# A new hand-laid order of the instructions on all five engines up to the last token tile, and a bit test of two transposes taken out, in a hybrid encoder layer on one core

## The chip, the cores and the metric

The kernel runs on one core of a Trainium2 chip. The metric is the device time of one execution in microseconds (us). Three runs of the kernel before gave 1298.33 us in the median (1297.25 to 1299.77). Everything that the engines do is in float32; a matmul is made of three passes over rounded high and low halves of its operands.

## The reference

One layer of an encoder is computed for nine token tiles: eight of 128 frames of a new stream, and one of 64 frames that continue a running stream with 512 cached positions.

```python
x <- LayerNorm(ALPHA * x + Mixer(x))          # D_MODEL = 1024
x <- LayerNorm(ALPHA * x + SqReLU_MLP(x))     # D_FF = 4096

Mixer: z = x @ w_in, its columns split among
  fox   6 heads x 64   causal softmax attention, logit += c_t - c_s, c = cumsum(log f)
  sgu   256 channels   u * (tril(W_s) @ LayerNorm(gelu(v)) + b) within 128 positions
  sb    6 heads x 64   strictly causal stick-breaking attention
  o = per-head RMSNorm of [fox, sgu, sb];  o @ w_out

def sq_relu_mlp(x, w_up, w_down):
    h = jnp.square(jax.nn.relu(x @ w_up))
    return h @ w_down
```

The new rows of keys, values and log gates are outputs too.

## The kernel before, in words

The program has four stages, one after the other but overlapping at their edges: the input projections with the two attentions and the gating (up to some 496 us of the profile), the output projection of one token tile after another, called mix (to some 607 us), the up projection, and the down projection, whose end also writes the outputs.

- **Projections.** `tok_mm` (L655) multiplies a transposed token tile `xT` by a slice of `w_in` into a PSUM bank. Its outputs are named `kvfox`, `qfox`, `kvsb`, `qsb`, `sgv` and so on. `x_trans` (L603) transposes the tiles of x that were loaded at L593 into buffers called `row_N`; `load_w` loads a weight slice (L624, `raw`) and splits it into halves (L628). The stores of new keys and values (L765, L766) come from `kvsfox`.
- **Attention.** A unit `b` is one head for one 256-row block of queries. Its scores `Sfox` or `Ssb` are made at L854, the row work follows on VectorE, ScalarE and GpSimd, and then the steps in `b_steps` run: `tr(m)` transposes blocks of weights into the PSUM tile `pt` (L903, the names `ptfox` and `ptsb`), VectorE splits `pt` into two halves `pth`, and `av(m)` multiplies these by the values into `ofox` or `osb` (L924 to L927). For two of the units, `fox1_1_0` and `sb1_1_0`, and only for m = 1, `tr` also makes a **test**: one block is transposed a second time in another number format (`same`, L907), VectorE takes the difference to the first, squares and sums it (`df`, L909 to L912), and adds the sum, times 2 to the 80th, to `negh` (L913), a small column that the unit uses elsewhere. Equal bits add zero.
- **Mix.** L522 multiplies the merged heads of one token tile by `w_out`; `ORD` gives the order of the tiles, the last one is tile 7. LayerNorm and the transposition for the MLP follow tile by tile (`row6`, `xr`, `xo`).
- **Up projection.** It runs as seven products of half-size blocks in place of eight (a Strassen-like scheme). A `Chain` (p, s) makes the seven products of weight block p with token half s: s = 0 has 288 columns, s = 1 has 256. Its banks are `zA_s`, `zB_s`, `zC_s`, `zD_s` (the matmuls at L1626), ScalarE copies `zA` out to `sn` (L1637), VectorE forms the others (L1640 to L1646), then come the squared relu (L1658), four block sums (L1667 to L1670) and stores to `h_dr` in memory (L1671, L1672). The weights of p = 0 are the first tiles `wa`, `ws`, `oTb`, `row1r`, `row4r`; those of each later p are loaded by one transfer `wr<-w_up` (L1826) and split by ScalarE (L1564, L1857), VectorE and GpSimd (L316).
- **Storage.** Big buffers lie in `row_N` places that are used again by later tiles. So `sn` of the chains after p = 0 lies where the `row` buffers of the last chain of p = 0, (0,1), lay: ScalarE can fill it only when the store of that buffer to `h_dr` has landed.

What sets the order: the program is recorded in full, and then each engine's instructions are chained in the order that the table `ORDER[engine]` gives, as words "n+k" (n times: take element k of those that are left). It is an order only, with no waiting beside it: an instruction starts when its engine has come to it and the data are there. SP's table orders the transfers that its queue issues, which stand behind each other in the same way.

Of the kernel before, what the change touches and what calls it, by code (L numbers as in the profile page):

```python
# [13 lines left out]
F32 = mybir.dt.float32  # L14
F32R = mybir.dt.float32r
AF = mybir.ActivationFunctionType
ALU = mybir.AluOpType
AX = mybir.AxisListType
# [3 lines left out]
P = 128  # L22
# [252 lines left out]
def _build(nc, tc, a, es):  # L275
# [23 lines left out]
    ident = cp.tile([P, P], F32, name="ident")  # L299
# [2207 lines left out]
```

## Time and profile before

| | |
|---|---|
| median of three runs | 1298.33 us |
| profiled execution, its own time | 1299.34 us |
| its span | 1297.6 us |
| TensorE (PE) busy | 1268.3 us, 98% |
| VectorE (DVE), ScalarE (ACT), GpSimd (POOL) busy | 966.8, 723.7, 602.5 us |
| mean granted TensorE clock | 0.995 |

The profiled execution is 1.0 us longer than the median, and 1.74 us of it lie outside the span. In the page, PE is the matmul engine, PEld its weight loads, which overlap, and SP the engine that issues most transfers (its queue is SPq in the trace). A timeline row gives the start in us, the time from the first start to the last end, the engine, the source line, the operation with its output and inputs, the shapes, the number of instructions in the row, and in brackets how long the engine had been idle and what released it. Matmuls are pipelined, so the start of one to the start of the next is the time that it takes.

### The profile page before, as it was taken

The page shows a single profiled execution, that of the slowest core. Times are in us where ns is not written, and L with a number is a line of the kernel's source. Part 1 is how long each engine was busy: PE and PEld are TensorE (multiplying, and loading weights), DVE is VectorE, ACT ScalarE, POOL GpSimd, SP SyncE. Part 2 cuts the span into 40 slices and gives each one's busy share as a digit, 9 for nine tenths or more (in the row PEclk, how much of TensorE's full clock was granted, in tenths as well). Part 3 has the DMA queues.
Part 4 walks back from the last instruction along what each step waited for, and adds up shares of the span by engine and source line. Part 5 has one row for each costly group of instructions (what it writes and reads, how often), then busy time and mean ns, then how long its engine had stood idle before and what let it go on. Part 6 is the DMA issues. An engine that isn't in the chain of part 4 may idle for free.

```text
span 1297.6 us, 24367 instructions
## 1 busy us (share of the span) xinstructions
PE 1268.3 (98%) x8853; PEld 1175.2 (91%) x8853; DVE 966.8 (75%) x1812; ACT 723.7 (56%) x1560; POOL 602.5 (46%) x670
## 2 busy tenths in 40 slices
PE   8999999999999999999899999999999999999996
PEld 8999999999989997778899999999988888888885
DVE  5678676778885687898678766766797667676777
ACT  4467676677675674344333222222367676676775
POOL 2232323257684666866122212121287656555567
PEclk9999999999999999999899999999999999999999
DMA  7445674322314376432324443535577443434433
GB/s 239 117 145 152 189 215 118 85 69 75 75 30 98 93 247 221 143 114 80 111 95 153 152 151 124 178 100 181 201 265 257 141 140 132 152 129 148 150 121 134
DMA packets 158049, 185.64 MB, mean 143 GB/s; under 512 B 27741, under 2 KB 116125, under 8 KB 157929
## 3 DMA queue, kind: packets, MB, share of 16 engines
q1 hardware_dynamic: 155832, 183.01, 44.5%
q8 instruction: 70, 1.15, 0.4%
q10 hardware_dynamic: 2096, 1.07, 0.3%
q14 instruction: 51, 0.41, 0.1%
HBM read 117.65 MB, written 60.10 MB: 137 GB/s over the span
## 4 chain that ended last, share of the span: by engine, by line
PE 79%; DVE 6%; POOL 5%; DMA 4%; issue 2%; ACT 2%; SPq 1%; DVEq 0%; POOLq 0%; ACTq 0%
PE A L2103 12%; PE zA L1626 11%; PE zD L1626 7%; PE D L2103 6%; PE kvsb L655 6%; PE kvfox L655 4%; PE zC L1626 4%; PE zB L1626 4%; PE B L2103 3%; PE Sfox L854 2%; PE mx L522 2%; PE qsb L795 2%; PE Ssb L854 2%; PE qfox L795 2%; PE sgu L655 1%
## 5 line engine op out<-in xcount | busy, mean ns | idle before, releaser
L316 POOL TENSOR_TENSOR wa<-wr,wa 128x512 fp32r<-128x512 f32 x41 | 56.6, 1403 | 233.1 <-ACT wa L1564 233.1
L316 POOL TENSOR_TENSOR wd<-rd,wd 128x512 fp32r<-128x512 f32 x77 | 104.0, 1361 | 109.2 <-ACT wd L1564 95.6
L1626 PE MATMUL zD<-xo,ws 128*128 128x288 f32 (+1 forms) x720 | 122.2, 287 | 0.1
L1626 PE MATMUL zA<-xo,ws 128*128 128x256 f32 (+1 forms) x720 | 113.1, 289 | 5.2 <-ACT sn L1637 5.2
L1626 PEld LDWEIGHTS zA<-xo,ws 128*128 128x128 f32 x720 | 99.5, 190 | 5.5 <-ACT sn L1637 5.5
L1626 PEld LDWEIGHTS zD<-xo,ws 128*128 128x128 f32 x720 | 102.9, 189 | 0.4 <-DVE hh L1640 0.4
L1637 ACT ACTIVATE sn<-zA 128x256 f32<-128x256 f32 (+1 forms) x80 | 30.8, 392 | 127.3 <-PE zA L1626 108.6
L522 PE MATMUL mx<-xT,oTb 128*128 128x512 f32 (+1 forms) x416 | 99.9, 394 | 1.0 <-DVE oTb L316 0.9
L655 PE MATMUL kvfox<-wkvfox,xT 128*128 128x256 f32 (+3 forms) x624 | 92.2, 289 | 2.5 <-DVE fx L758 1.3
L2103 PE MATMUL A<-wd,wd 128*128 128x512 f32 x312 | 94.2, 389 | 0.0
L522 PEld LDWEIGHTS mx<-xT,oTb 128*128 128x128 f32 (+1 forms) x416 | 75.6, 186 | 18.9 <-DVE oTb L316 1.7
L840 POOL TENSOR_TENSOR row<-row,row 128x127 f32<-128x127 f32 (+8 forms) x51 | 64.3, 1262 | 42.8 <-DVE row L838 34.2
L655 PEld LDWEIGHTS kvfox<-wkvfox,xT 128*128 128x128 f32 (+1 forms) x624 | 80.8, 187 | 3.1 <-DVE fx L758 1.5
L655 PE MATMUL kvsb<-wkvsb,xT 128*128 128x256 f32 (+1 forms) x624 | 79.7, 281 | 0.0
L1758 POOL TENSOR_TENSOR rd<-rd 128x512 f32<-128x512 f32 x56 | 73.3, 1310 | 10.1 <-DVE b L316 6.2
L2103 PE MATMUL A<-wd,h4a 128*128 128x512 f32 x240 | 77.7, 389 | 0.0
L838 DVE TENSOR_TENSOR_SCAN row<-row,one 128x128 f32<-128x128 f32 (+8 forms) x51 | 71.8, 1411 | 4.5 <-ACT row L837 3.4
L655 PEld LDWEIGHTS kvsb<-wkvsb,xT 128*128 128x128 f32 (+1 forms) x624 | 74.9, 186 | 0.0
L1564 ACT ACTIVATE wd<-rd 128x512 fp32r<-128x512 f32 x105 | 63.4, 621 | 17.3 <-POOL rd L1758 7.9
L2103 PEld LDWEIGHTS A<-wd,wd 128*128 128x128 f32 x312 | 58.6, 188 | 12.9
L2070 DVE TENSOR_TENSOR acc<-acc,A 128x512 f32<-128x512 f32 x73 | 49.6, 684 | 25.3 <-PE A L2103 24.8
L1626 PE MATMUL zB<-xo,wa 128*128 128x288 f32 (+1 forms) x360 | 66.5, 288 | 0.0
(729 smaller groups left out, 3861.6 us busy)
## 6 DMA issues: line engine op xcount, KB each, us to landing
h_dr<-hh SPq DMA_DIRECT2D x30, 512.0 KB, 3.2
rd<-w_down SPq DMA_DIRECT2D x30, 512.0 KB, 4.4
wr<-w_up SPq DMA_DIRECT2D x13, 1024.0 KB, 5.6
hr<-h_dr SPq DMA_DIRECT2D x31, 384.0 KB, 3.2
h_dr<-hh SPq DMA_DIRECT2D x30, 384.0 KB, 3.1
raw<-w_in SPq DMA_DIRECT2D x42, 256.0 KB, 3.2
wo_dr<-swo SPq DMA_DIRECT2D x32, 256.0 KB, 2.3
xT<-wo_dr SPq DMA_DIRECT2D x8, 1024.0 KB, 7.6
```

The lines of the kernel that those rows point to most:

```text
L316: eng.tensor_tensor(out, src, hi.bitcast(F32), op=ALU.subtract)
L522: nc.tensor.matmul(acc[0:m], oT[:, k, hx, 0:m], wo[k // 4][hw][:, k % 4, cs], start=(i == 0), stop=(i == len(seq) - 1))
L655: nc.tensor.matmul(acc[0:n, c0:c0 + n1 - n0], xT[k // 4][:, k % 4, c:c + n], wt[:, k, hw, n0:n1], start=(i == 0), stop=(i == len(seq) - 1))
L795: nc.tensor.matmul(acc[:, 0:w], wq[:, k, hw, :], xT[k // 4][:, k % 4, c:c + w], start=(i == 0), stop=(i == len(seq) - 1))
L838: nc.vector.tensor_tensor_scan(g[:, 0:n][:, ::-1], g[:, 0:n][:, ::-1], one.broadcast_to([P, n]), 1.0, op0=ALU.mult, op1=ALU.bypass)
L840: nc.gpsimd.tensor_tensor(s[:, 0:n - 1], s[:, 0:n - 1], g[:, 1:n], op=ALU.mult)
L854: nc.tensor.matmul(sps[:, b0 - c0:b0 - c0 + n], qd[:, h, s, half * P:(half + 1) * P], kp[b0 // 256][:, h, 0:n], start=(s == 0), stop=(s == ...
L1564: nc.scalar.activation(hi, raw, AF.Copy)
L1626: nc.tensor.matmul(z, w[:, hw, k], xop(s, bo, hx)[:, k, :], start=(new and k == 0 and j == 0), stop=(k == 3 and j == 2), skip_group_check= ...
L1758: eng.tensor_tensor(r[:, o], r[:, x], r[:, y], op=ALU.subtract)
L2070: nc.vector.tensor_tensor(out, out if other is None else other, bank, op=ALU.add)
L2103: nc.tensor.matmul(z, h[:, hx, q, o], wset[self.c % 2][q][:, hw, wb], start=((n in (0, 3) or n == 1 and self.c == 0) and q == 0 and j == 0 ...
```

## The change

The `ORDER` tables of all five engines are written anew, for the part of the program up to the last token tile. The rest of each table gives the order of before: from 706 us of the old profile on, every engine's order is the same. 5047 of the 8851 matmuls stand at another place, and 883 VectorE, 698 ScalarE, 341 GpSimd and 414 SP instructions do. The test in `tr` is gone, and with it two transpositions on PE and ten VectorE instructions. The changed file is six lines longer in all; lines behind the table are numbered 17 higher than before, and behind the test 6 higher.

```diff
 ORDER = {}
-14 2+10 +12 1 +11 2+9 1 +8 1 +7 21 +14 2+10 +12 3+10 1 +9 +33 +36 1 2+32 +33 +32 2 2+6 +28 1 7+5 +51 1 +46 +19
...
                         nc.tensor.transpose(ptr[:, bi * P:(bi + 1) * P], rows[half][1][:, kb * P:(kb + 1) * P], env["identr"])
-                    if nm in ("fox1_1_0", "sb1_1_0") and m == 1:
-                        at = len(traced)
-                        same = ps.tile([P, P], F32, name=f"same{nm}", tag="o", bufs=1)
-                        nc.tensor.transpose(same, rows[0][0][:, 2 * P:3 * P], ident)
-                        df = sa.tile([P, P + 1], F32, name=f"df{nm}", tag="df", bufs=1)
-                        nc.vector.tensor_copy(df[:, 0:P], same)
-                        nc.vector.tensor_tensor(df[:, 0:P], pt[:, 0:P], df[:, 0:P], op=ALU.subtract)
-                        nc.vector.tensor_tensor(df[:, 0:P], df[:, 0:P], df[:, 0:P], op=ALU.mult)
-                        nc.vector.tensor_reduce(df[:, P:P + 1], df[:, 0:P], axis=AX.X, op=ALU.add)
-                        nc.vector.scalar_tensor_tensor(negh, df[:, P:P + 1], 2.0 ** 80, negh, op0=ALU.mult, op1=ALU.add)
-                        apart.update(i.name for i in traced[at:])
...
-        left = [i for i in traced[from_here:] if i.engine == e.engine and "Boundary" not in type(i).__name__ and i.name not in apart]
+        left = [i for i in traced[from_here:] if i.engine == e.engine and "Boundary" not in type(i).__name__]
```

**The seam between the first weight block and the second, on PE.** In these names the first number behind `zB_`, `zA_` and so on is the half s. `oTb` and `row1r` are weights of p = 0 and `wa`, `ws` are weights of p = 1, and `xo` is the transposed input. Before, the last product of chain (0,1), zD, ends the work on p = 0:

```order
L1626 MATMUL zC_1_9013<-xo_8723,row1r 128x256 x4
L1626 MATMUL zD_1_8979<-xo_8722,oTb 128x256
L1626 MATMUL zA_1_9182<-xo_8722,wa_8922 128x256 x3
L1626 MATMUL zD_1_8979<-xo_8722,oTb 128x256 x11
L1626 MATMUL zA_1_9182<-xo_8722,wa_8922 128x256 x2
L1626 MATMUL zD_0_9119<-xo_7969,ws_9010 128x288 x2
L1626 MATMUL zB_0_9092<-xo_7969,wa_8922 128x288 x2
L1626 MATMUL zC_0_9146<-xo_7969,wa_8922 128x288
L1626 MATMUL zA_0_9076<-xo_7969,ws_9010 128x288
```

Now, from the same last product on:

```order
L1632 MATMUL zD_1_8963<-xo_8706,oTb 128x256 x12
L1632 MATMUL zC_0_9130<-xo_7953,wa_8906 128x288 x3
L1632 MATMUL zC_1_9249<-xo_8707,wa_8906 128x256 x2
L1632 MATMUL zB_0_9076<-xo_7953,wa_8906 128x288 x2
L1632 MATMUL zC_1_9249<-xo_8707,wa_8906 128x256
L1632 MATMUL zC_0_9130<-xo_7953,wa_8906 128x288
L1632 MATMUL zA_1_9166<-xo_8706,wa_8906 128x256
L1632 MATMUL zB_0_9076<-xo_7953,wa_8906 128x288
```

The row `zA_0<-xo,ws`, the third product of chain (1,0), stood 7 matmuls behind the last zD of p = 0; it now stands 61 matmuls behind it, and the matmuls between belong to the first products of both chains of p = 1 and to the parts of zB, zC and zD that need no `sn`.

**The same seam on VectorE.** `row_116` and `row_110` belong to chain (0,1), `h_0` to chain (0,0), `ws_9010` and `ws_8994` are weights of p = 1. Before:

```order
L316 TENSOR_TENSOR ws_9010<-row_92,ws_9010 128x8x128
L1642 TENSOR_TENSOR row_116<-zB_1_8952,sn_1_0_8929 128x256
L1646 TENSOR_TENSOR row_110<-zD_1_8979,sn_1_1_8930 128x256
L1658 SCALAR_TENSOR_TENSOR row_116<-row_116 128x512
L1658 SCALAR_TENSOR_TENSOR row_110<-row_110 128x512
L1668 TENSOR_TENSOR h_0_8798<-h_0_8798 128x256
L1667 TENSOR_TENSOR row_116<-row_110 128x256
L1668 TENSOR_TENSOR row_116<-row_116 128x256
L1669 TENSOR_TENSOR h_0_8798<-h_0_8798 128x256
L1670 TENSOR_TENSOR row_110<-row_116,row_110 128x256
L1669 TENSOR_TENSOR row_110<-row_116 128x256
```

Now:

```order
L1664 SCALAR_TENSOR_TENSOR row_116<-row_116 128x512
L1652 TENSOR_TENSOR row_110<-zD_1_8963,sn_1_1_8914 128x256
L1664 SCALAR_TENSOR_TENSOR row_110<-row_110 128x512
L1673 TENSOR_TENSOR row_116<-row_110 128x256
L1674 TENSOR_TENSOR row_116<-row_116 128x256
L1675 TENSOR_TENSOR row_110<-row_116 128x256
L1676 TENSOR_TENSOR row_110<-row_116,row_110 128x256
L1674 TENSOR_TENSOR h_0_8782<-h_0_8782 128x256
L333 TENSOR_TENSOR ws_8994<-row_80,ws_8994 128x8x128
L1675 TENSOR_TENSOR h_0_8782<-h_0_8782 128x256
```

The relu of `row_116` and its zB and zC sums moved ahead of the last zD, the two sums of `h_0` moved behind those of chain (0,1), and the two `ws` splits moved from ahead of these steps to behind them. On ScalarE, the transfer `wr<-w_up` of the next weight block stood behind the first copy `sn_0`; it now stands behind two copies, `sn_0` and `sn_1`.

**Transposes on PE.** The names `ptfox_2_1_0` and `ptfox_2_1_1` are blocks of one unit. Before, they stand one by one among the matmuls:

```order
L903 MATMUL ptfox_2_1_0_1521<-identr,row4r 128x128
L854 MATMUL Sfox_6_0_512_1588<-kpfox_3_553,qdfox_3_1130 128x128
L926 MATMUL ofox_2_0_1302<-pthfox_2_0_1_1367,vpfox_1_350 128x256
L927 MATMUL ofox_2_0_1302<-pthfox_2_0_1_1367,vpfox_1_350 128x256
L924 MATMUL ofox_2_0_1302<-pthfox_2_0_2_1411,vpfox_2_453 128x256
L925 MATMUL ofox_2_0_1302<-pthfox_2_0_2_1411,vpfox_2_453 128x128
L903 MATMUL ptfox_2_1_1_1549<-identr,row4r 128x128
L655 MATMUL kvfox_7_1485<-wkvfox_720,xT_181 128x256
```

Now:

```order
L871 MATMUL Sfox_7_0_512_1609<-kpfox_2_452,qdfox_3_1130 128x256 x2
L920 MATMUL ptfox_2_1_1_1549<-identr,row4r 128x128
L920 MATMUL ptfox_2_1_1_1549<-identr,row3r 128x128
L920 MATMUL ptfox_2_1_2_1572<-identr,row4r 128x128
L920 MATMUL ptfox_2_1_2_1572<-identr,row3r 128x128
L672 MATMUL kvfox_8_1814<-wkvfox_720,xT_181 64x256
```

Up to the last matmul of mix, the PE order of before has 399 runs of one or more transposes between matmuls, 200 of them a single transpose; the order of after has 329 runs, 155 of them single.

**The start of SP's queue.** `x_prompt` and `w_in` rows are loads; `p_fox_k` rows are stores of computed keys. Before:

```order
L593 DMA row_86<-x_prompt 128x1024
L593 DMA row_80<-x_prompt 128x1024
L624 DMA raw_0_244<-w_in 128x4x128
L678 DMA bf_654<-b_f 128x6
L678 DMA bf_908<-b_f 128x6
L624 DMA raw_1_248<-w_in 128x4x128
```

Now:

```order
L610 DMA row_86<-x_prompt 128x1024
L695 DMA bf_908<-b_f 128x6
L782 DMA p_fox_k<-kvsfox_0_294 128x128
L610 DMA row_116<-x_prompt 128x1024
L641 DMA raw_0_244<-w_in 128x4x128
L782 DMA p_fox_k<-kvsfox_1_341 128x128
L610 DMA row_80<-x_prompt 128x1024
L783 DMA p_fox_v<-kvsfox_0_294 128x128
L783 DMA p_fox_v<-kvsfox_1_341 128x128
L782 DMA p_fox_k<-kvsfox_2_397 128x128
```

The load of `row_80`, a later tile of x, now stands behind the stores of the first two computed key tiles.

410 rows, old and new, of the table ORDER are left out of this document.

## The prediction

> **What bounds the kernel now.** I read the page's busy shares first.
>
> ```profile
> PE 1268.3 (98%) x8853; PEld 1175.2 (91%) x8853; DVE 966.8 (75%) x1812; ACT 723.7 (56%) x1560; POOL 602.5 (46%) x670
> ```
>
> PE is the bound; no engine beside it is above 75%. A table by stage shows how much PE leaves open, and where (columns: length, then busy time of PE, PEld, DVE, ACT and POOL, the clock, the DMA share, GB/s).
>
> ```profile
> 0.00:607.00 607.00, 593.61 (x4660) 563.87 (x4661) 457.03 (x984) 369.87 (x882) 301.17 (x419) 1.00 0.45 131
> 635.00:647.00 12.00, 6.75 (x33) 6.52 (x32) 3.81 (x10) 0.67 (x2) 0.00 (x0) 0.72 0.70 230
> 647.00:706.00 59.00, 59.00 (x481) 59.00 (x480) 45.95 (x64) 17.62 (x33) 12.39 (x9) 1.00 0.38 123
> 706.00:1287.00 581.00, 580.87 (x3460) 518.56 (x3460) 426.99 (x698) 315.92 (x609) 274.57 (x225) 1.00 0.47 158
> ```
>
> From 647 us PE has no gap, and from 706 us nothing is moved. What a new order can win lies in two places: 607.00 - 593.61 = 13.4 us of idle PE up to 607, and 12.00 - 6.75 = 5.25 us in the 12 us at the seam of the first two weight blocks, where the clock is 0.72 besides. Busy time can shrink too, if the same matmuls follow each other at shorter distances. The waits of PE in 0 to 610 us (total, times, longest) are many and small: 23 rows, with a sum of 12.5 us, of which these matter.
>
> ```profile
> PE warm L1402 <- POOL ident masks.py:199: 1.6, 1, 1.6
> PE kvfox L655 <- DVE fx L758: 1.3, 1, 1.3
> PE kvfox L655 <- ACT wkvfox L628: 1.2, 1, 1.2
> PE osb L924 <- ACT osbsb L937: 1.0, 1, 1.0
> PE mx L522 <- DVE row3a L527: 0.2, 1, 0.2
> ```
>
> **A: the seam.** The timeline of PE, with those of ACT and POOL, the piece of the chain that PE waits for, and the transfers of `w_up` that follow (count, size, median us to land):
>
> ```profile
> 628.45 1.58 PE L1626 MATMUL zA<-xo,oTb 128*128 128x256 f32 x12
> 629.86 0.28 PE L1626 MATMUL zD<-xo,oTb 128*128 128x256 f32 x1
> ...
> 633.54 1.41 PE L1626 MATMUL zD<-xo,oTb 128*128 128x256 f32 x11
> 634.79 0.39 PE L1626 MATMUL zA<-xo,wa 128*128 128x256 f32 x2
> 635.54 0.29 PE L1626 MATMUL zC<-xo,wa 128*128 128x288 f32 x1
> 641.09 0.61 PE L1626 MATMUL zA<-xo,ws 128*128 128x288 f32 x1 [5.25 <-ACT sn L1637]
> 643.65 1.40 PE L1626 MATMUL zA<-xo,ws 128*128 128x288 f32 x5
> 644.85 0.44 PE L1626 MATMUL zC<-xo,wa 128*128 128x288 f32 x1
> 646.53 0.29 PE L1626 MATMUL zB<-xo,wa 128*128 128x256 f32 x1
> ```
> ```profile
> 637.41 0.43 DVE row L1668
> 637.86 2.61 DMA h_dr<-row
> ...
> 640.62 0.41 ACT L1637 ACTIVATE sn<-zA 128x288 f32<-128x288 f32 x1 [7.82 <-DMA h_dr<-row]
> 640.78 0.39 ACTq L1826 DMA_DIRECT2D wr<-w_up  x1
> 648.16 1.16 ACT L1564 ACTIVATE wa<-wr 128x512 fp32r<-128x512 f32 x2 [1.01 <-DMA wr<-w_up]
> 649.45 1.28 POOL L316 TENSOR_TENSOR wa<-wr,wa 128x512 fp32r<-128x512 f32 x1 [24.35 <-ACT wa L1564]
> ...
> wr<-w_up SPq DMA_DIRECT2D x3, 1024.0 KB, 5.6
> ```
>
> After the last product of p = 0, which is through at about 634.9, PE has 7 matmuls that do not need `sn`, and then stands until 641.09. The chain of release is: last zD, relu and sums on VectorE (row L1668), the store (2.61 us to land), the copy `sn` into the place that it frees. From zD's end to zA that is 641.09 - 634.9 = 6.2 us. The gap costs twice: 5.25 us idle, and then matmuls of 288 columns 0.24 us apart ((644.85 - 643.65) / 5), where in ordinary work 256 columns take 0.117 (12 in 629.86 - 628.45) and 288 by the same rate 0.132. Of these, (646.53 - 641.09) / 0.24 = 23 lose 0.11 each, 2.5 us. Together 7.7 us (5.25 + 2.5).
>
> The Trainium skill, in "TensorE: Matmul & The Clock Gate", Part 1: The HAM clock gate, says that an idle window of about 3.4 us halves the clock and that as much of sustained work restores it. The trace agrees on the fall after 5.25 us idle and on none after 1.3 us; its return took 5.4 us here.
>
> In the new order 61 matmuls stand in the 7 matmuls' place: 61 x 0.123 (between both widths) = 7.5 us of work against a need of 6.2. So 1.3 us are to spare, more since two sums of `h` stand ahead of the store no longer, and both costs go: -7.7.
>
> What is late next is the weight load behind `sn`: it is issued on ScalarE's queue 5.9 us after zD's end before (640.78), and behind the copy of `sn_1` now, whose matmuls end 67 behind zD (67 x 0.123 = 8.2 us), so with the copy's 0.41 at about +8.7. It took 648.16 - 640.78 = 7.4 us to the first split, then 1.16 on ACT and 1.28 on POOL. Its first use stands 127 matmuls behind zD, 127 x 0.123 = 15.6 us; the hi half would be there at +8.7 + 7.4 + 0.6 = +16.7, 1.1 late, and POOL's half 1.28 behind it, at +18.0, where the order first uses it 142 matmuls behind zD, +17.5. So PE may stand for some 1.1 us; a landing as fast as 5.6 us, the median of the loads after it, would make it nothing. I take +1.0. A = -6.7, with ends of -7.7 and -2 (R1 below).
>
> **B: transposes side by side.** Around a lone transpose in the attention:
>
> ```profile
> 93.65 0.35 PE L927 MATMUL ofox<-pthfox,vpfox 128*128 128x256 f32 x1
> 93.84 0.23 PE L903 MATMUL ptfox<-identr,row4r 128*128 128x128 f32 x1
> ...
> 93.97 0.35 PE L854 MATMUL Sfox<-kpfox,qdfox 128*128 128x256 f32 x1
> 94.15 0.22 PE L903 MATMUL ptfox<-identr,row3r 128*128 128x128 f32 x1
> ```
>
> The 256-column matmul behind a transpose holds PE 0.19 and 0.18 us, against 0.117 in a row of its kind: about 0.06 us for each run of transposes, however many it holds. By my count of the two orders up to the end of mix there are 399 runs before and 329 after. B = -70 x 0.06 = -4.2 us. Its ends: 0 if the extra time belongs to each transpose and only its place moves, and -6.
>
> **C: the test.** Its VectorE steps and the PE instructions that stand behind them:
>
> ```profile
> 138.38 0.29 DVE L909 COPY dffox<-samefox 128x128 f32<-128x128 f32 x1 [0.97 <-PE samefox L907]
> 139.56 0.55 DVE L316 TENSOR_TENSOR pthfox<-ptfox,pthfox 128x384 fp32r<-128x384 f32 x1
> 139.66 0.39 PE L854 MATMUL Sfox<-kpfox,qdfox 128*128 128x256 f32 x2
> 140.82 0.47 PE L854 MATMUL Sfox<-kpfox,qdfox 128*128 128x256 f32 x2 [0.78 <-PE Sfox L854]
> 343.53 0.27 PE L907 MATMUL samesb<-ident,row 128*128 128x128 f32 x1
> 344.18 0.39 PE L924 MATMUL osb<-pthsb,vpsb 128*128 128x256 f32 x1 [0.38 <-DVE dfsb L909]
> ```
>
> Four `df` instructions hold VectorE from 138.38 to 139.56, 1.2 us, and the split and the score step behind them come that much later. PE pays 140.82 - 139.66 less 0.23 for two matmuls = 0.93 there, 344.18 - 343.53 less 0.11 for the transposition = 0.54 at the second test, and the two transpositions themselves, 0.2. C = -1.7. Its ends: -0.2 if other waits fill both gaps, and -2.4, twice the 1.2 us that VectorE is held. VectorE's other 966 us have cover, PE being the bound.
>
> **D: the other waits up to 607 us.** Of the 13.4 us idle, the 1.6 at `warm` and 1.2 at the first weights come before any order counts; 1.2 (0.78 and 0.38) are in C. The 1.3 at `fx` should go: by the order the matmuls between the two uses of that bank grow from 0.9 to 2.4 us of work. Of the 8 that are left most single waits get more work ahead of them, but the number of matmuls that carry a wait grows from 731 to 762, and two places (the gating at 370 to 400, the end of attention at 489 to 496) stay as tight as they are. I take half the 8 as gone and as much as 2 as opened: D = -1.3 - 4 + 2 = -3.3, with ends of +8 (each wait replaced twice) and -9.
>
> **Sum.** -6.7 - 4.2 - 1.7 - 3.3 = -15.9 from 1299.34 is 1283.4; the profiled execution lies 1.0 above the median of the runs, so 1282.4 against 1298.33. Since a new order is likelier to have unseen waits than unseen gains, I say 1283.
>
> **Rivals.**
> R1, the seam only shrinks. For it: the wait for the late `wr` load, which stands behind one more copy; against it the 1.3 us to spare and the median of 5.6 us. A stop of 1.3 us (`fx`) brought no slow stretch and one of 5.25 did; if one half way, 3.3 us, is left and brings it too, A = -7.7 + 3.3 + 2.5 = -2, and the time is 1283 + 4.7 = 1288. By the Trainium skill's rule, named above, 3.3 us would be just too short to lose the clock, and the time 1285.
>
> R2, the order moves the waits instead of closing them, D = +5 and B half: 1283 + 8.3 + 2.1 = 1293. For it: 5047 moved matmuls, 31 more of them with a wait; against it, PE already runs with 98% of its time busy, and small waits are short here.
>
> R3, slower: SP's queue. Loads stand behind stores that wait for computed keys (first row: the loads of x, with their median time to land).
>
> ```profile
> row<-x_prompt SPq DMA_DIRECT2D x8, 512.0 KB, 6.4
> ...
> 3.39 2.93 SPq L593 DMA_DIRECT2D row<-x_prompt  x5
> ...
> 16.96 0.39 ACT L756 ACTIVATE kvsfox<-kvfox 128x256 f32<-128x256 f32 x1
> 22.32 0.37 PE L603 MATMUL xtp<-identr,row6r 128*128 128x128 f32 x3
> ```
>
> Five x tiles are issued by 6.3 us now. In the new order the tile `row_80` waits for a store of the keys copied at 16.96 to 17.35, and the second half of the next weights for one tile more. It then has from 17.4 to 22.3 to land before transposes like those in the last row; with the 6.4 us that the eight x loads take in the median, and its rounding by another 1 or so, PE waits 2 to 3 us, and for each later load of that kind as long. Slower it gets when this repeats at seven loads or more ((15.9 + 2.6) / 2.7). With ten it is 1283 + 27 = 1310. Against it: the transfers take a share of 0.45 up to 607 us, so that landings later on have room, and the new order still lists the loads of later weights far ahead of their use.
>
> R4, more than thought: D = -9 and B = -6, 1275.
>
> **How the numbers follow.** 0.2% (2.6 us) is about what a measurement of this kernel can tell from no change. Chances: the sum as forecast (1278 to 1287) 0.45; R1 (to 1290) 0.15; R2 (1288 to 1296) 0.22; R3 0.10, of which 0.07 beyond 1301; R4 0.08. Faster takes the forecast, R1, R4 and 0.20 of R2: 0.88; same 0.05, slower 0.07. The range leaves out R3 and the ends of R2 and R4: 1276 to 1294.
>
> **What would show it.** A right: in the trace of after, no wait of zA for `sn` at about 625 us, clock 1.00 in every slice, and at most a 2 us wait on a `wa` step some 16 us behind the last zD. B right: PE's busy time up to mix falls by about 4 us with the same matmuls. C right: no `df` row, and no wait of Sfox or osb in those units above 0.3. D right: idle PE ahead of mix's end at about 7 to 8 us, without the `fx` wait. Wrong it would be by a wait on `xtp` or `kvfox` for DMA in the first 40 us, a clock dip elsewhere, or more than 12 us idle up to mix's end.

## The result, and the profile after

The changed kernel took 1288.02 us in the median of four runs (1287.42 to 1288.30), against 1299.05 us before (four runs, 1297.25 to 1300.32): a ratio of 0.9915, with a 95% interval of 0.9898 to 0.9933. That is 11.0 us faster, inside the predicted range, where 15.3 us had been forecast. The profiled execution took 1287.42 us, its span is 1285.7 us.

The page's busy shares, and the 12 us that hold the seam (columns as in the prediction's table):

```profile
PE 1260.6 (98%) x8851; PEld 1170.1 (91%) x8851; DVE 970.5 (75%) x1802; ACT 723.7 (56%) x1560; POOL 606.1 (47%) x670
```
```profile
625.00:637.00 12.00, 12.00 (x101) 12.00 (x100) 10.05 (x20) 1.94 (x4) 0.00 (x0) 1.00 0.45 158
```

The seam at 625 to 637 us has no idle time and full clock. To compare the two kernels over the same work, the next rows go from the start to the last token tile of mix, where both have done the same 4617 matmuls (the two transpositions of the tests not counted), and from there to the 5431st, behind the seam. Before comes first, then after:

```profile
0.00:597.73 597.73, 584.34 (x4620) 556.18 (x4620) 448.52 (x970) 366.55 (x877) 295.80 (x414) 1.00 0.45 133
597.73:710.77 113.04, 107.43 (x815) 105.27 (x814) 89.09 (x139) 40.02 (x74) 31.40 (x27) 0.97 0.36 117
```
```profile
0.00:592.76 592.76, 578.65 (x4618) 553.24 (x4618) 450.41 (x953) 365.82 (x876) 297.46 (x414) 1.00 0.46 134
592.76:697.84 105.08, 105.01 (x816) 103.00 (x815) 84.76 (x144) 40.65 (x75) 31.97 (x27) 1.00 0.38 126
```

The stretch with the seam is 113.04 - 105.08 = 8.0 us shorter. Ahead of it 5.0 us were won, and they are busy time: PE is busy 584.34 - 578.65 = 5.7 us less, but idle 592.76 - 578.65 = 14.1 us, where it was 597.73 - 584.34 = 13.4 us before. The waits of PE in 0 to 700 us show what stands where the old waits stood (19 rows; total, times, longest):

```profile
PE kvfox L672 <- DVE wkvfox L643: 2.3, 1, 2.3
PE sgv L672 <- DVE sgvv L1076: 1.5, 3, 0.8
PE sgv L672 <- ACT so L1127: 1.4, 1, 1.4
PE sgm L1123 <- DVE qdsb L823: 0.9, 1, 0.9
```

The wait for `fx` and the waits of the two tests are gone, and those at the first weights and in the gating (`sgv`, `sgm`) have grown. Because PE takes its matmuls in a fixed order, there are places at which both orders have done the same set of them, again without the tests' two; the table gives the start of the next matmul there, and how far after is ahead.

| matmuls done | place | before, us | after, us | lead of after, us |
|---|---|---|---|---|
| 46 | first weights | 9.7 | 10.5 | -0.9 |
| 286 | behind the `fx` wait | 39.3 | 37.7 | +1.5 |
| 2077 | second attention begins | 249.1 | 245.5 | +3.6 |
| 3053 | gating | 365.3 | 362.0 | +3.3 |
| 3512 | behind the gating | 423.7 | 422.8 | +0.9 |
| 4093 | end of attention | 493.5 | 490.3 | +3.2 |
| 4617 | last token tile of mix | 597.7 | 592.8 | +5.0 |
| 5431 | behind the seam | 710.8 | 697.8 | +12.9 |
| 8700 | down projection | 1253.0 | 1241.0 | +12.0 |

The seam gives 8.0 us of it. From 39 us to the seam 3.5 us come, where 4.2 (transposes), 1.7 (tests) and about 2 (other waits) had been forecast. Of the 12.9 us, 0.8 are lost again by 716 us of before, in the part where no order differs: there after has a stop that before does not have,

```profile
703.63 1.86 PE L1632 MATMUL zA<-xo,ws 128*128 128x288 f32 x12 [0.55 <-ACT sn L1643]
```

at a copy `sn` for which ScalarE comes late, behind a split of `ws`. No run was made on this stop.

### The profile page after: what moved, and what is told of

Same layout as the page of the kernel before. It is cut to its first block, busy times and chain, and to the rows that moved or that the text cites. A ratio compares the mean times of both kernels' runs of the same rounds, so it can differ in the third digit from the quotient of the medians.

```text
span 1285.7 us, 24330 instructions
## 1 busy us (share of the span) xinstructions
PE 1260.6 (98%) x8851; PEld 1170.1 (91%) x8851; DVE 970.5 (75%) x1802; ACT 723.7 (56%) x1560; POOL 606.1 (47%) x670
## 4 chain that ended last, share of the span: by engine, by line
PE 69%; DVE 4%; POOL 2%; ACT 2%; DMA 1%; issue 1%; DVEq 0%; SPq 0%; ACTq 0%; POOLq 0%
PE A L2109 13%; PE zA L1632 10%; PE zD L1632 7%; PE D L2109 6%; PE mx L539 6%; PE kvsb L672 4%; PE zC L1632 3%; PE zB L1632 3%; PE B L2109 3%; PE sgu L672 2%; PE Ssb L871 2%; PE qsb L812 1%; PE sgv L672 1%; PE ds L2155 1%; PE ds L2153 1%
## 5 line engine op out<-in xcount | busy, mean ns | idle before, releaser
L1632 PE MATMUL zD<-xo,ws 128*128 128x256 f32 (+1 forms) x720 | 126.0, 287 | 0.1
L1632 PE MATMUL zA<-xo,ws 128*128 128x288 f32 (+1 forms) x720 | 115.0, 287 | 0.5 <-ACT sn L1643 0.5
L672 PE MATMUL kvfox<-wkvfox,xT 128*128 128x256 f32 (+3 forms) x624 | 96.7, 287 | 2.5 <-DVE wkvfox L643 2.3
L672 PE MATMUL kvsb<-wkvsb,xT 128*128 128x256 f32 (+1 forms) x624 | 98.6, 287 | 0.0
L672 PEld LDWEIGHTS kvsb<-wkvsb,xT 128*128 128x128 f32 (+1 forms) x624 | 83.9, 187 | 0.1
L2109 PEld LDWEIGHTS A<-wd,wd 128*128 128x128 f32 x312 | 58.6, 188 | 12.9
L1632 PE MATMUL zB<-xo,wa 128*128 128x288 f32 (+1 forms) x360 | 69.5, 287 | 0.0
```

Source lines behind the costliest of these rows:

```text
L672: nc.tensor.matmul(acc[0:n, c0:c0 + n1 - n0], xT[k // 4][:, k % 4, c:c + n], wt[:, k, hw, n0:n1], start=(i == 0), stop=(i == len(seq) - 1))
L1632: nc.tensor.matmul(z, w[:, hw, k], xop(s, bo, hx)[:, k, :], start=(new and k == 0 and j == 0), stop=(k == 3 and j == 2), skip_group_check= ...
L2109: nc.tensor.matmul(z, h[:, hx, q, o], wset[self.c % 2][q][:, hw, wb], start=((n in (0, 3) or n == 1 and self.c == 0) and q == 0 and j == 0 ...
```

## The experiments

The kernels below are made from the changed one by other `ORDER` tables. "The old order" means the relative order that before gives the same instructions; all have the tests taken out. Each was timed against before on its own chip.

**The test alone.** All five tables in the old order:

```diff
-ORDER[engine] = <after>
+ORDER[engine] = <before>     # tests out, nothing else moved
```

> The order of before on all engines, with the two tests taken out and nothing else moved. Theory of the prediction: VectorE is free 1.2 us earlier twice, and PE gets 0.93 + 0.54 us of waits and 0.2 us of transpositions back: 1.7 us below before, some 1297.3. Rival: the units wait for something else just as late, and the time stays that of before, 1299.0. The waits of Sfox and osb in the two units tell them apart in the trace whatever the time says.

Measured: 1298.49 us against 1298.91, ratio 0.9994 (0.9983 to 1.0004). The waits of PE between 140 and 350 us in this kernel:

```profile
PE wstp L1083 <- POOL row L1071: 0.7, 1, 0.7
PE ofox L904 <- DVE otsfox L1037: 0.4, 1, 0.4
PE otpsb L925 <- ACT osbsb L917: 0.2, 1, 0.2
PE kvfox L646 <- ACT kvsfox L747: 0.2, 1, 0.2
PE otpfox L925 <- ACT osbfox L917: 0.2, 1, 0.2
```

and in before, from 130 us:

```profile
PE Sfox L854 <- PE Sfox L854: 0.8, 1, 0.8
PE osb L924 <- DVE dfsb L909: 0.4, 1, 0.4
PE pkfox L778 <- DVE otfox L946: 0.3, 1, 0.3
PE otpsb L945 <- ACT osbsb L937: 0.2, 1, 0.2
```

Both sum to 1.7 us. The stops of the test went, and as much came up behind them: `wstp` waits for GpSimd, `ofox` for another VectorE step. The leads at equal work say the same. The kernel with the test out wins 1.0 us at the first test (from 2.1 us behind to 1.1 behind, at 141 us of before) and has lost it by 159 us; it wins 1.4 at the second, and 0.9 of it is gone at the next matmul but one, the `wstp` above. By the times alone the forecast 1.7 us would still lie within the interval, so it is the trace that speaks for the rival: most of what each stop cost is given back within 20 us.

**The seam alone, and the seam undone.** The new order only from 607 us on, and the mirror:

```diff
+e2: order of before for what started by 607 us, then order of after
+e3: order of after for what started by 602.4 us, then order of before
```

> The order of before on all engines for all that had started by 607 us of its profile, the order of after behind that; the tests are out. Theory: the seam is worth its whole price by itself, 5.25 us of stop and 2.5 us of half clock, so 7.7 to 8.3 us less than the same kernel with the old seam, about 1289.3, with no wait of zA for sn and a clock of 1.00 there. Rival: the 12 us that after won are spread over the program and the seam needs the earlier lead of after too; then no more than 4 us less, 1293.

> The mirror: the order of after for all that had started by 602.4 us of its profile, the order of before behind that. Theory: the wait of zA for sn comes back with 5 us or more, the matmuls behind it run at half rate for some 5 us, and the time is 7.7 to 8.3 us above after, about 1296. Rival: the lead that after has by then covers part of it, 1292.

Measured: the seam alone gives 1290.12 us against 1298.91 before (0.9930, 0.9916 to 0.9944) and 1298.49 for the same kernel with the old seam: 8.4 us. Undone, the kernel takes 1298.57 us (0.9994, 0.9981 to 1.0006), so all that the rest of the new order gave is lost beside it. In the profile of the seam alone it wins 8.3 us on before between the 4617th and the 5431st matmul, where after wins 8.0. The seam is also nearly the whole change: after came out at 0.9915 of before, and at 0.9931 when it was run again (below), and the seam alone at 0.9930. By the times, all that was rewritten ahead of the seam is thus worth 0 to 2 us, with intervals of 2 to 3 us either way; the two profiles, with 12.0 - 8.0 = 4.0, show more. In the kernel with the seam undone the wait is back:

```profile
635.39 0.61 PE L1633 MATMUL zA<-xo,ws 128*128 128x288 f32 x1 [5.26 <-ACT sn L1644]
```

That profiled execution is its shortest, 1293.2 us; the others have a mean clock of 0.988 to 0.993 against 0.995, and take 4 to 10 us more. Where their clock was low no trace shows, so of the 10 us by which the median lies above after, only some 8 are explained.

**What takes the stop away, and how long a stop halves the clock.** One matmul of after is moved, and all other engines keep its order:

```diff
 L1632 MATMUL zD_1_8963<-xo_8706,oTb 128x256 x12
 ... (7 or 30 matmuls)
+L1632 MATMUL zA_0_9060<-xo_7953,ws_8994 128x288
 ... (to 61 matmuls behind zD)
-L1632 MATMUL zA_0_9060<-xo_7953,ws_8994 128x288
```

> After, with one matmul moved: the first zA with ws, which waits for sn, stands 30 matmuls behind the last zD of p = 0 in place of 61. In the trace of after, sn was copied out 6.85 us behind zD's end, so PE stops for 6.85 - 30 x 0.123 = 3.2 us. Theory R1 of the prediction, by the rows: a stop of that length halves the clock too, and the time is 3.2 + 2.5 above after, 1293.7. Rival, by the Trainium skill, TensorE: Matmul & The Clock Gate, Part 1: The HAM clock gate: under 3.4 us the clock stays, and the time is 1291.2.

> The same matmul 7 behind zD, as it stood before; VectorE, ScalarE, GpSimd and SP keep the order of after. Theory: what took the stop away is the work of PE ahead of zA alone; the stop is 6.85 - 0.9 = 6 us and the slow stretch follows: 8.5 above after, 1296.5. Rival: the new order on VectorE and the queues is what made the release early; then the stop is no more than 3 us, 1291.

The unaltered kernel ran beside them:

> The changed kernel once more, unaltered, to have it on the same chip as the others: 1288.0 is expected.

Measured: after 1289.89 us here (1285.73 to 1295.87; 0.9931, 0.9909 to 0.9953), with 30 matmuls ahead 1294.47 (0.9958, 0.9946 to 0.9971), with 7 1296.97 (0.9984, 0.9974 to 0.9995). The waits are as expected, 3.08 and 5.85 us, first with 30 and then with 7:

```profile
636.66 0.43 PE L1637 MATMUL zA<-xo,ws 128*128 128x288 f32 x1 [3.08 <-ACT sn L1648]
```
```profile
635.67 0.61 PE L1637 MATMUL zA<-xo,ws 128*128 128x288 f32 x1 [5.85 <-ACT sn L1648]
```

So the work that PE has in hand took the stop away; VectorE's new order alone did not bring the release early enough. The clock, in windows of 2 us (the third number from the end), first with 30 matmuls ahead, then in before:

```profile
636.00:638.00 2.00, 1.34 (x6) 1.34 (x7) 1.23 (x1) 0.61 (x2) 0.00 (x0) 0.72 1.07 342
638.00:640.00 2.00, 2.00 (x10) 2.00 (x10) 0.00 (x0) 0.00 (x0) 0.00 (x0) 0.50 0.06 8
640.00:642.00 2.00, 2.00 (x18) 2.00 (x17) 0.00 (x0) 0.00 (x0) 0.00 (x0) 0.92 0.00 0
```
```profile
638.00:640.00 2.00, 0.00 (x0) 0.00 (x0) 0.84 (x3) 0.00 (x0) 0.00 (x0) 0.93 0.67 270
640.00:642.00 2.00, 0.92 (x4) 0.92 (x5) 0.00 (x0) 0.41 (x1) 0.00 (x0) 0.50 1.00 347
642.00:644.00 2.00, 2.00 (x10) 2.00 (x10) 0.00 (x0) 0.00 (x0) 0.00 (x0) 0.50 0.95 226
644.00:646.00 2.00, 2.00 (x10) 2.00 (x9) 0.00 (x0) 0.00 (x0) 0.00 (x0) 0.50 1.05 352
646.00:648.00 2.00, 2.00 (x17) 2.00 (x16) 0.00 (x0) 0.41 (x1) 0.00 (x0) 0.86 0.93 281
```

The missing clock adds up to (0.28 + 0.50 + 0.08) x 2 = 1.7 us after a stop of 3.08, which is 3.4 us at half rate, and to (0.07 + 0.50 + 0.50 + 0.50 + 0.14) x 2 = 3.4 us, twice that, after 5.25. But a low clock costs only while PE works: in before it began at 639.7 and PE came back at 641.09, so 1.4 of the 6.8 us at half rate lie inside the stop, and (6.8 - 1.4) / 2 = 2.7 us were lost. With the 5.25 that makes 8.0, what the seam was worth in the leads. The second piece does not come every time: of six profiles with a stop of over 5 us five have 6.8 us at half rate behind it, and the one of the kernel with the test out, whose stop at the seam was 5.26, has 3.4. A stop of 3.1 us costs 1.7 us more than itself: 4.6 us were measured, 4.8 by these rows. For the stop of 5.85 us, 2.0 of whose 6.8 us at half rate lie inside it, the same sum gives 5.85 + 2.4 = 8.3 us; the medians are 7.1 apart, which the spread of the runs of after, 10 us, leaves open.

**Transposes cut apart.** In after, 70 runs of transposes are cut in two:

```diff
 <transpose>
-<transpose>
 <matmul>
+<transpose>
 <matmul>
```

> After, with 70 of its runs of transposes cut in two: the last transpose of a run changes places with the matmul behind it, which gives the 398 runs of before in place of 328 and moves no other instruction. Theory: each run costs 0.06 us, so 4.2 us more than after, 1292.2, all of it as busy time of PE without new waits. Rival: the extra time belongs to each transpose, or the gaps lie in waits anyway, and the time stays at 1288.0.

Measured: 1291.22 us (0.9935, 0.9921 to 0.9949). Its interval overlaps that of after, but the profiles, both with the same low clock at the gating and none ahead of it, tell more: with the same matmuls done this kernel is behind after by 0.6 us at 916 matmuls, 2.2 at 2077 and 3.0 at 5431. How much of it is busy time, up to these 5431 matmuls, first in after, then here:

```profile
0.00:697.84 697.84, 683.66 (x5432) 656.24 (x5433) 535.17 (x1096) 406.48 (x951) 329.43 (x440) 1.00 0.45 133
```
```profile
0.00:700.88 700.88, 685.86 (x5432) 658.62 (x5433) 535.72 (x1096) 405.52 (x951) 328.92 (x440) 1.00 0.45 132
```

PE is busy 685.86 - 683.66 = 2.2 us longer, and the other 0.8 are waits that grew. Theory and rival lie on both sides: a run costs 2.2 / 70 = 0.03 us of busy time, not 0.06 and not nothing.

**The start.** First the new start with the old order behind it, then the old start with the new order:

```diff
+e10: order of after for what started by 41.9 us, then order of before
+e8:  order of before for what started by 9.0 us, then order of after
```

> The order of after for all that had started by 41.9 us of its profile, that of before for the rest; the tests are out. In the two profiles PE has done the same 320 matmuls 1.4 us earlier in after at this place: 1.0 us later through the first weights, 2.4 earlier behind the wait for fx. Theory: 1.4 us under the kernel with the old start, 1297.1. Second theory: in two profiles the old start's stop at fx, of 1.5 and 2.2 us, was followed by 5 us of lower clock, in the third of 1.3 it was not; if the old start loses 2 us in about half of its executions, the new one is 2.4 us under it in the median, 1296, and its times spread less.

> The order of before for what had started by 9.0 us of its profile (the first loads and weights), that of after for all the rest. In five profiles of the order of after at this place PE stops for 2.3 us ahead of the first weights, 1.0 more than in before, and in four of the six that have it the clock then is at half for 3.4 us, 1.7 us lost. Theory: without this stop and without the one at fx both prices go, 1.0 us always and 1.7 in most executions: 2 to 2.7 us under after, some 1287.5 where after has 1289.9, with no clock below 1.00 up to 60 us. Rival: PE meets a later landing a few us on and stops there; then the same time as after.

Measured: the new start alone is worth nothing, 1299.08 us (0.9997, 0.9985 to 1.0009), and its times spread as before, from 1294.2 to 1302.4. The old start with the new order behind it takes **1284.12 us** (1283.67 to 1285.61; 0.9892, 0.9879 to 0.9906), the shortest of all kernels here. Two stops that it lacks bear on that. One is the `fx` wait of the old order; the profile of the kernel with the test out shows it longer than before, and the clock behind it:

```profile
27.36 1.86 PE L646 MATMUL kvfox<-wkvfox,xT 128*128 128x262 f32 x9 [2.18 <-DVE fx L749]
```
```profile
28.00:30.00 2.00, 2.00 (x11) 2.00 (x11) 0.40 (x2) 0.64 (x2) 0.84 (x2) 0.50 0.75 220
30.00:32.00 2.00, 2.00 (x14) 2.00 (x14) 1.36 (x3) 0.49 (x2) 0.00 (x0) 0.65 0.04 8
```

In two of three profiles with the old order there the clock fell (not in before's own). The other is the wait at the first weights in the new order, here in the unaltered after on the second chip:

```profile
9.79 0.48 PE L677 MATMUL kvfox<-wkvfox,xT 128*128 128x262 f32 x2 [2.33 <-DVE wkvfox L648]
```
```profile
10.00:12.00 2.00, 2.00 (x12) 2.00 (x12) 2.00 (x4) 0.00 (x0) 0.00 (x0) 0.56 0.63 235
12.00:14.00 2.00, 2.00 (x14) 2.00 (x13) 0.17 (x1) 0.00 (x0) 0.00 (x0) 0.59 0.35 76
```

The clock fell behind it in four of seven profiles, each time by (0.44 + 0.41) x 2 = 1.7 us or nearly so. What PE waits for is the split `wkvfox<-raw` on VectorE. Before, VectorE makes it first, as soon as the load has landed. In the new order it stands behind a split of `row` and one of `xT`, and starts 2.0 us later without having waited for a load itself (before, then after):

```profile
6.19 0.43 DVE L626 CAST wkvfox<-raw 128x512 fp32r<-128x512 f32 x1 [3.42 <-DMA raw<-w_in]
```
```profile
7.59 0.69 DVE L333 TENSOR_TENSOR xT<-xtp,xT 128x512 fp32r<-128x512 f32 x1 [0.53 <-ACT xT L622]
8.20 0.42 DVE L643 CAST wkvfox<-raw 128x512 fp32r<-128x512 f32 x1
```

SP's queue changed there too, with one `row<-w_in` ahead of the two `raw` halves; no run separates the two. In the profile of the old start with the new order neither stop is there, up to 60 us:

```profile
0.00:9.00 9.00, 7.29 (x41) 7.04 (x42) 4.03 (x11) 4.43 (x8) 2.34 (x17) 1.00 0.86 257
9.00:60.00 51.00, 50.41 (x431) 49.48 (x431) 31.66 (x78) 22.68 (x60) 11.91 (x24) 1.00 0.57 164
```

By the leads this kernel is 1.0 us ahead of after behind the first weights and 1.8 at the end, in profiles of which neither has a fall of the clock at the start. By the times it is 3 to 5 us under after, each against before on its own chip; the stop, and 1.7 us of half clock behind it in some executions, could make up 1.0 to 2.7 of that, and the rest is not traced.

**The gating.** Between 365 and 424 us after loses 2.4 of its 3.3 us of lead. Its profile stops twice there, and the clock falls behind it:

```profile
394.84 0.33 PE L932 MATMUL osb<-pthsb,vpsb 128*128 128x128 f32 x1 [0.68 <-DVE pthsb L333]
...
396.21 0.48 PE L1123 MATMUL sgm<-row6r,wst 128*128 128x256 f32 x2 [0.88 <-DVE qdsb L823]
```
```profile
396.00:398.00 2.00, 1.79 (x11) 1.61 (x12) 1.87 (x6) 1.88 (x5) 1.45 (x3) 0.79 0.00 0
398.00:400.00 2.00, 2.00 (x13) 2.00 (x12) 1.73 (x4) 0.66 (x2) 0.94 (x4) 0.50 0.62 101
400.00:402.00 2.00, 2.00 (x17) 2.00 (x17) 0.69 (x1) 1.19 (x3) 0.71 (x1) 0.86 0.64 169
```

Again 1.7 us. Of the seven profiles with these two stops six have the fall; the one of the seam undone, with stops of 0.66 and 0.88 us, has not. Two kernels put the old order there, on top of the old start, and a third exchanges two VectorE rows:

```diff
+e9:  order of before from 248 us (after) to 534 us (before)
+e11: order of before from 325 us (after) to 470 us (before)
 e12: on DVE, ahead of sgm7:
-L1074 g1v8 ...
 L823 qdsb2_0 ...
+L1074 g1v8 ...
```

> As the last, and besides the order of before from 248 us (after's profile) to 534 us (before's), where the two profiles' lead of after shrinks from 3.95 to 2.62 us although the second test is gone; after's order again behind that. Theory: the waits of the gating in after's order, with the 1.7 us of half clock behind them at 396 to 402 us in each of its profiles, are part of where the expected gain went, and the sum is 2.5 us under the last kernel, 1285. Rival: the fewer runs of transposes that after has there are worth as much as its waits cost, and it is the same time.

> As the last, with the order of before only from 325 us (after's) to 470 us (before's), so that the end of the attention, where one of six profiles with the old order there had two low stretches of 3.4 us, is after's. Theory: the gating holds the loss, so this is within 1 us of the last kernel or better, without a low clock between 380 and 500 us. Rival: the join at 470 us, where the two orders have not done the same work, brings a stop of its own.

> e8_start_old with two neighbours on VectorE exchanged: the split qdsb ahead of the step on g1v, for which VectorE stood 0.41 us at 394.2. In its profile sgm at 395.67 waited 0.88 us for that split, behind a stop of 0.67, and the clock then was at half for 3.4 us. sgm now waits for row6r on ScalarE, done at 394.94. Theory: the second stop shrinks to 0.2 us, PE's clock stays at 1.00 between 395 and 402, and the time is 0.7 + 1.7 = 2.4 us below e8_start_old, 1281.8. Rival: the clock falls from the short distances between the transposes and the first stop alone; then 0.7 us less, 1283.5.

Measured: the first took 1293.44 us (0.9964, 0.9950 to 0.9977), a miss that tells nothing of the gating, because the join at 248 us made a stop of its own:

```profile
256.15 2.07 PE L802 MATMUL qsb<-xT,wqsb 128*128 128x256 f32 x8 [6.85 <-DVE qdsb L813]
```

The second took 1285.69 us (0.9902, 0.9888 to 0.9916): no gain over the old start alone. Its profile has no low clock at 396, but two others of 1.7 us, at 165 to 175 and, behind a wait of 1.34 us for `so` within the old order's gating, at 370 to 380. The third took 1285.56 us (0.9893, 0.9876 to 0.9911), no gain either. The second stop shrank to 0.18 us, as expected, but the clock fell all the same:

```profile
398.77 0.50 PE L1128 MATMUL sgm<-row6r,wst 128*128 128x256 f32 x2 [0.18 <-ACT row6r L1160]
399.60 0.39 PE L1128 MATMUL sgm<-row3r,wst 128*128 128x256 f32 x1 [0.33 <-POOL row3r L338]
```
```profile
400.00:405.00 5.00, 4.91 (x31) 4.71 (x30) 3.56 (x8) 2.81 (x7) 2.75 (x4) 0.66 0.45 107
```

So stops of 0.67, 0.18 and 0.33 us within 2 us, with a stretch of transposes and narrow matmuls around them, were enough there. This profile, the longest of its four runs, has a second low stretch of 1.7 us at 373 to 377, behind another stop of 0.67. That the gating costs after its lead is read off the traces; no kernel here won it back, so how to win it stays open.

## Why the prediction was right, point by point

The time came into the range because the seam did what A said. That it lies no further than 5 us from the 1283 us forecast is in part luck, because the other terms were wrong in both directions and offset each other. In us, by the two profiles at equal work:

| term | forecast | found |
|---|---|---|
| A, the seam | -6.7 | -8.0 |
| B, busy time up to the seam | -4.2 | -7.2 |
| C and D, the tests and the idle time up to the seam | -5.0 | +0.5 |
| half clock in the gating | none | +1.7 |
| lost again behind the seam | none | +1.0 |
| sum | -15.9 | -12.0 |

Two of the prediction's own signs of being wrong came: more than 12 us idle up to mix's end (14.1), and a dip of the clock elsewhere, in the gating. R1's figure, 1288, is the measured time by chance; the stop that R1 keeps at the seam is gone.

- **A, the seam: -6.7 forecast, -8.0 measured by the leads and -8.4 by the runs.** The mechanism was as told, and the moved part of the PE order alone carries it. The price was right too: 5.25 us of stop, and 2.7 for the slow stretch where 2.5 were counted. What was off is the +1.0 for the late `wr` load, which was not paid; its landing took 5.4 us, not the 7.4 of before, and no wait stands at its first use. The margin was smaller than said, since ScalarE's `sn` stood behind the split of `ws`: the copy started at 635.05 and its successor 61 matmuls behind zD at 636.10, 0.65 us after the copy ended, not 1.3.

```profile
634.09 1.06 ACT L1863 ACTIVATE ws<-row 128x1024 fp32r<-128x1024 f32 x1 [8.01 <-DVE row L1583]
635.05 0.39 ACT L1643 ACTIVATE sn<-zA 128x288 f32<-128x288 f32 x1
637.11 0.38 ACTq L1832 DMA_DIRECT2D wr<-w_up  x1
642.58 1.15 ACT L1570 ACTIVATE wa<-wr 128x512 fp32r<-128x512 f32 x2 [0.19 <-DMA wr<-w_up]
```

- **B, the transposes: -4.2 forecast; -3.0 when 70 runs are put back, 2.2 of it busy time.** The price of a run, read off one neighbourhood, was twice too high. By the busy times of the two profiles up to the seam more was won: 5.7 us less, of which 0.2 are the tests' transposes, while the gating's slow stretch adds 1.7; that leaves 7.2. So some 5 us of the shorter busy time are not the number of runs, and no run here shows what they are.
- **C, the test: -1.7 forecast, none found in the trace.** The end named for it, other waits that fill the gaps, is what happened. Time taken from one engine ahead of a stop is not PE's time until the next release is seen to be early too.
- **D, the other waits: -3.3 forecast, a loss measured.** `fx` went as told. But idle PE up to the last token tile rose by 0.7 us (13.4 to 14.1), though C had put 1.5 and D 3.3 on its fall: the first weights cost 1.0 more, and the waits of `sgv` and `sgm` for the gating grew from 1.5 to 4.8 us. The step that failed is that a wait with more work ahead of it goes and few new ones open. Beside it stands a price that the sum did not have at all, 1.7 us of half clock at the gating, and again at the first weights in some executions. These two lost more than the 15.3 - 11.0 = 4.3 us that are missing; A and B made up for a part.
- **R1** was priced from stops of 1.3 and 5.25 us, with a fall assumed half way. At 3.08 us the clock did fall, so by that part the rows were right and 3.3 us would not have been safe. **R2** is what D became, at half its price. **R3** did not come: none of PE's 19 waits is for a load of x, and the stop at the first weights is for a split on VectorE, ahead of any store of keys.

## What to carry to other kernels

When a new order is weighed, the big wait with its release chain can be sized to a microsecond, and it carries the result; the sum of small waits could not here, because those that were taken away showed others. Compare two orders where PE has done the same set of matmuls: such points gave the loss in the gating and at the start, and the old first loads ahead of the new order gave a kernel some 4 us under the changed one (1284.1 against 1288.0 and 1289.9 us, each on a chip of its own). Count the work that both have done with care: an instruction that only one of them has must be left out. For a stop of TensorE from 1.5 us on, price 1.7 us or more beside the stop itself, as a risk, since stops of 1.5 to 2.3 us halved the clock in some executions of these kernels and not in others. And run the big term alone early: the seam by itself gave 0.9930 of before, where the whole change gave 0.9915 and 0.9931.

## What the runs showed of the hardware

The low clock came in pieces of 3.4 us at half rate, or of twice that; where PE was at work all the while, a piece of 3.4 us cost 1.7. Twice that came behind five of the six stops of over 5 us, and in the profile of the seam alone, its longest run, behind a stop of 1.64 us at the end of the attention. The Trainium skill, "TensorE: Matmul & The Clock Gate", Part 1: The HAM clock gate, says that the clock returns after about 3.4 us of sustained work, and the length of these pieces agrees. It also says that it takes an idle window of about 3.4 us to lose it, and that differs: the clock fell behind stops of 1.54 and 2.18 us at `fx`, of 2.33 us at the first weights in four of seven profiles, and of 0.67, 0.18 and 0.33 us at the gating, but not behind 1.34 us at `fx` in before. It also fell behind the 3.08 us at the seam, ahead of which only matmuls of the up projection run. The stop of 1.54 us, and the window behind it, from the kernel with the new seam alone:

```profile
26.79 2.17 PE L651 MATMUL kvfox<-wkvfox,xT 128*128 128x262 f32 x9 [1.54 <-DVE fx L754]
```
```profile
28.00:30.00 2.00, 2.00 (x11) 2.00 (x10) 0.27 (x1) 0.90 (x2) 0.26 (x1) 0.50 0.49 142
```

In each of these places but the seam transposes run ahead of the stop. The Trainium skill, "TensorE: Matmul & The Clock Gate", Part 4: PE-mode transpose, says that a transpose does not count as work in the same way, which would make these stops longer than they look; no run here separates that from the stop itself, so it stays open.
